# A hybrid decoder block on one core: how meta and x come in, and where the second residual is stored

## The chip, the cores and the metric

The kernel runs on one core of a Trainium2 chip. The core has a matrix engine (TensorE, PE in the profile), a vector engine (VectorE, DVE), a scalar engine (ScalarE, ACT), GpSimd (POOL), and the queues of SyncE (SP), ScalarE and GpSimd, from which transfers are started. The metric is device time in microseconds, the median of several runs. All times below are in microseconds where no unit stands.

## The reference

One layer works on 16 learned meta tokens followed by 256 tokens of x, each of 2048 channels. Everything is in float32. Cut to what matters:

```python
h = concatenate([meta, x])                       # 272 x 2048
u = rms_norm(h, g_pre_mix)
z_pool, v_conv, g_conv, gate_a, gate_b = split(u @ w_in)
y_a = causal_multiscale_pool(z_pool, w_pool_grp, pool_scale) @ w_pool_out
y_b = conformer_conv(v_conv, g_conv, w_dw, ...) @ w_conv_out
m = sigmoid(gate_a) * y_a + sigmoid(gate_b) * y_b
h = h + rms_norm(m @ w_o, g_post_mix)
u = rms_norm(h, g_pre_mlp)
h = h + rms_norm(square(relu(u @ w_up)) @ w_down, g_post_mlp)
return h without the meta tokens
```

## The kernel before, in words

**Precision.** A float32 product is made of three products of rounded parts. Each weight and each activation is split in a high part (a cast on ScalarE) and a low part, the residue (a subtraction on VectorE); high times high, high times low and low times high are added up in PSUM. So each weight chunk of 1 MB (128 x 2048) costs a transfer, a cast and a residue before TensorE can use it.

**The start.** Tokens have to stand in the free dimension and channels on partitions, so x and meta are turned by TensorE (a product with the identity, `ident`). At the start SP loads meta as 16 rows (`m_in`, L433), ScalarE's queue and SP load the first 512 columns of x in two halves of 128 tokens (L436), and then SP loads the first two weight chunks in pieces (`open_chunk`, L351), with the rest of x in three pieces of 512 columns between them (`X_BEHIND`, `load_x`). A third chunk follows whole. `DUMMIES` says how many turns of the identity onto itself `keep_warm` issues in three places. `meta_tiles` turns meta by sixteen products (L498), multiplies by the gain (L502) and splits it (L507, L508) in four parts, the first before the loop and three in it. `x_tile(k)` turns channel tile k, two products (L488), and splits it (L490 on ScalarE, L491 on VectorE). `pieces_to` splits the weights' rows for it (L356, L359). The first loop has sixteen steps, one for each channel tile, of six products (L534) each; tiles 0 to 2 are turned before it, and step k turns tile k + 3 behind its products. From step 5 on, every second step squares a piece of x or meta for the first norm (`sq_tile`, L516); the squares left over are planned. GpSimd's queue loads the taps and the parameter rows after the last piece of x is there (L442 to L444).

**The planned parts.** All that follows is put down as a list of items, each with an engine, a cost, and the names of what it reads and writes (`plan.add`). TensorE's order is given; from it each item gets a due time, and `order` plays the list through and has every engine take the ready item that is due first. The order that comes out is the program. The first plan holds everything up to the output projection `w_o`. Its weight chunks are split by `split_of` (L817 on ScalarE, L822 on VectorE), one whole chunk at a time. The second plan holds the MLP, with its own loads (L1773) and splits (L1800, L1805).

**Between the two plans** an order is written out by hand. It ends the last block of `w_o`, forms `norm1` for the two halves of 128 tokens (t = 0, 1), adds the residual block by block (`residual(t, n)`, L1501, four blocks of 512 columns for each t), turns the sum `h1` (`u2_tiles`, L1577, with casts L1583 and residues L1587), and makes the first products of `w_up` (`up_high`, `up_low`). The second plan then begins with eight squares of h1 (`square_h1`, L1495 on ScalarE) for the second norm, and a single transfer of h1 to DRAM (`keep_h1`, L1778, 2 MB, on SP's queue). Only after it can the room of h1 be used for weights (rooms 5 and 6). The copy in DRAM comes back near the end for the last residual (L2126).

Of the kernel before, what the change touches and what calls it, by code (L numbers as in the profile page):

```python
# [28 lines left out]
LAST_PIECE = "U1a0 U1a1 U1b0 U1b1 X1 X2 Y1 Y3 Y2 Y4 X3 X4"  # L29


DUMMIES = (11, 2, 1)
SQUARES_FROM = 5
AFTER_G0 = [("z", 0), ("z", 1), ("v", 1), ("z", 2), ("g", 1), ("v", 2), ("g", 2), ("z", 3),
            ("v", 3), ("g", 3)]
# [175 lines left out]
def hybrid_block(ctx: ExitStack, tc: tile.TileContext, ins: dict, out: bass.AP):  # L211
# [212 lines left out]
    def col(name, k):  # L424
        return vecs[:, cols[name] + k:cols[name] + k + 1]

    X_BEHIND = {(0, 4): 1, (0, 8): 2, (1, 4): 3}

    def load_x(b):
        sl = slice(b * CW, (b + 1) * CW)  # L430
        nc.sync.dma_start(x_in[:, :, sl], xv[:, :, sl])

    nc.sync.dma_start(m_in, meta)  # L433
    pre_rows = load_rows(nc.scalar, "g_pre_mix")
    for t, queue in enumerate((nc.scalar, nc.sync)):
        queue.dma_start(x_in[:, t, :CW], xv[:, t, :CW])  # L436
    for _ in range(FIRST + 1):
        open_chunk()
    ssq = const.tile([P, NT + 1, XB], F32, name="ssq")
    taps_in = big.tile([TAPS, CC], F32, tag="c", name="taps_in")  # L440
    nc.gpsimd.memset(ssq, 1.0)
    nc.gpsimd.tensor_copy(taps_in[:, :1], x_in[:TAPS, 0, D - 1:])  # L442
    nc.gpsimd.dma_start(taps_in, w_dw)
    other_rows = load_rows(nc.gpsimd, "pool_scale", "b_dw", "conv_ln_g", "conv_ln_b", "g_pre_mlp")  # L444
    warm_up(AF.Sqrt)
# [3 lines left out]
    def keep_warm(n):  # L449
        for _ in range(n):  # L450
            nc.tensor.transpose(idle[:, :P], ident, ident)
# [41 lines left out]
            op0=ALU.mult, op1=ALU.subtract)  # L493

    def meta_tiles():
        pt = acc_tile("mt_in")[:, :KD * M].rearrange("p (k m) -> p k m", k=KD)
        for k in range(KD):
            nc.tensor.transpose(pt[:, k, :], m_in[:, k * P:(k + 1) * P], ident[:M, :M])  # L498
# [3 lines left out]
        nc.vector.tensor_mul(mt, pt, vecs[:, g0:g0 + KD, None].broadcast_to([P, KD, M]))  # L502

        def part(ks, i):
            hi, lo = u.meta(ks, 0)[i], u.meta(ks, 1)[i]
            src = mt[:, ks.start:ks.stop - 1, :] if i == 0 else mt[:, ks.stop - 1, :]
            nc.scalar.copy(hi, src)  # L507
# [61 lines left out]
    meta_parts = meta_tiles()  # L569
    first_banks = acc_tiles("v0", HALF_CW // P)  # L570
    accs = [acc[:, :L] for acc in first_banks]
    squares = [(b, t) for b in range(XB) for t in range(NT + 1)]
    LEAD = 3

    def turn_and_split(k):
        if k < KD:
            x_tile(k)
        pieces_to(k + 1)

    meta_parts.pop(0)()  # L580
    keep_warm(DUMMIES[1])
    for k in range(LEAD):
        turn_and_split(k)
    keep_warm(DUMMIES[2])
    for k in range(KD):
        for j, acc in enumerate(accs):
            mm3(acc, *opened[k // HALF[0]][:2], u, (k % HALF[0], k), slice(j * P, (j + 1) * P),
                k == 0, k == KD - 1)
        turn_and_split(k + LEAD)
        if k < 3:  # L590
            meta_parts.pop(0)()
        if k >= SQUARES_FROM and k % 2 and k < KD - LEAD:
# [27 lines left out]
    def block(n):  # L620
        return slice(n * CW, (n + 1) * CW)
# [189 lines left out]

    def split_of(m_, q, rows):
        box, n = split_at[m_], slot0 + m_

        def high():
            box["flat"] = part_tile("hi", n)
            nc.scalar.copy(box["flat"], rooms[q]())  # L817
            box["hi"] = box["flat"].rearrange("p (k c) -> p k c", k=rows)

        def low():  # L820
            lo = part_tile("lo", n)
            nc.vector.tensor_sub(lo, rooms[q](), f32(box["flat"]))  # L822
            box["lo"] = lo.rearrange("p (k c) -> p k c", k=rows)
        return high, low

# [663 lines left out]

    norm1 = Norm("mix")  # L1490
    norm3 = Norm("mlp")

    def square_of(src, norm, t, n, scale=1.0):
        junk = tmp.tile([P, CW], F32, tag="junk", bufs=1, name=f"sq_{norm}_{n}_{t}")
# [5 lines left out]
    def residual(t, n):  # L1500
        nc.vector.scalar_tensor_tensor(  # L1501
            h1[:, t, block(n)], og[:, t, block(n)], norm1.r[:, t], h1[:, t, block(n)],
            op0=ALU.mult, op1=ALU.add)

    def m_of(k):
        return lambda part, ts_: m[:, k, part, ts_]
# [97 lines left out]
    def last_block(t):  # L1604
        last_factor(og[:, t, block(NB - 1)], last_o[t], NB - 1)
# [2 lines left out]
    norm1.finish(0)  # L1608
    for n in range(2):
        residual(0, n)  # L1610
    last_block(0)

    def both(parts):
        high, low = parts
        high()
        for i in range(CK):
            low(i)
# [8 lines left out]
    chain[0]()  # L1626
    high()
    residual(0, 2)
    for i, f in enumerate(chain[1:]):
        f()  # L1630
        low(i)
# [20 lines left out]

    up_high(0, 0)
    both(u2_tiles(0, 1, 2 * CK, CK))
    up_high(1, 0)
    parts_ = u2_tiles(1, 1, 0, CK)
    residual(1, 1)
    both(parts_)
    up_high(2, 0)
    both(u2_tiles(1, 1, CK, CK))  # L1660
    residual(1, 2)
    last_block(1)
    residual(1, 3)
    residual(0, 3)
    ups[2][2].pop(0)()
    up_high(0, 1)
    up_low(0)
# [44 lines left out]
    kept = dram.tile([P, NT, D], F32, name="kept")  # L1712
    H_ROOMS = (5, 6)

    banks = {"u0": acc_tile("bank_u0"), "u1": acc_tile("bank_u1")}
    for j in range(4):
# [53 lines left out]
    def load(r):  # L1770
        src, (rows, width) = source(*r)
        room = room_at[r] = free_rooms.pop(0)
        plan.add("SP", 3.15 if r[0][0] == "U" else 2.95, lambda: nc.sync.dma_start(  # L1773
            room_of[room].rearrange("p (k c) -> p k c", k=rows), src),
            writes=(f"raw{room}",))

    def keep_h1():
        nc.sync.dma_start(kept, h1)  # L1778
# [58 lines left out]
    last_use_order = list(uses)  # L1837


    ssq2 = const.tile([P, NT, NB], F32, name="ssq2")  # L1840
    r2 = const.tile([P, NT], F32, name="r2")
    box2 = {}

    def square_h1(t, n):
        return lambda: square_of(h1[:, t, block(n)], ssq2, t, n)

    def mean2():
        box2["v"] = v = tmp.tile([P, NT], F32, tag="tot", name="tot2")
# [240 lines left out]
                 writes=(f"x{j // 2}{j % 2}",))  # L2089
    loads()  # L2090
    for t in range(NT):
        for n in range(NB):
            plan.add("ACT", 0.92, square_h1(t, n), writes=("junk", "ssq2"))
    plan.add("SP", 6.0, keep_h1, reads=("ssq2",), writes=[f"raw{r}" for r in H_ROOMS])
    free_rooms += H_ROOMS
    loads()
    plan.add("DVE", 0.4, mean2, reads=("ssq2",), writes=("v2",))
# [143 lines left out]
```

## Time and profile before

| | us |
|---|---|
| median of three runs | 1182.91 |
| the three runs | 1181.7, 1182.91, 1183.52 |
| profiled execution | 1181.75 |
| its span, first to last instruction | 1179.6 |

The profiled execution is 2.15 longer than its span. TensorE is busy for 1167.2 of the span, VectorE for 1064.4, ScalarE for 706.8 and GpSimd for 62.3. The first product of the first loop starts at 8.03, the first product of the third weight chunk at 23.88; the hand-written order runs from about 492 to 530, and h1 is stored from 536.27 on.

In the timeline a row has the start, the length, the engine, the line, the operation, what it writes and reads, and how many alike are merged; a bracket has the idle time before it and what ended it. "PEld" is TensorE's loading of the stationary operand, "SPq" and "ACTq" are the issuing of transfers.

### The profile page before, as it was taken

What the parts mean: (1) busy time and instruction counts of PE and PEld (TensorE: products, weight loads), DVE (VectorE), ACT (ScalarE), POOL (GpSimd) and SP (SyncE); (2) the same over time, 40 slices, a digit from 0 to 9 for tenths busy, and PEclk for the clock granted to TensorE, in tenths of its full rate; (3) what the DMA queues carried; (4) which work ended last, traced back from release to release, by engine and by line L of the source; (5) the groups of instructions that cost most, each with busy time, mean ns of one, the idle gap of its engine ahead of it and who ended that gap; (6) DMA issues with size and microseconds to landing.
All of it is one profiled execution on the core that took longest, in us unless ns stands there. A gap on an engine that the chain in (4) does not pass through costs nothing.

```text
span 1179.6 us, 15795 instructions
## 1 busy us (share of the span) xinstructions
PE 1167.2 (99%) x6314; PEld 1013.1 (86%) x6314; DVE 1064.4 (90%) x1155; ACT 706.8 (60%) x718; POOL 62.3 (5%) x62
## 2 busy tenths in 40 slices
PE   9999999999999999999999999999999999999996
PEld 9999998788888888898888888888888888888885
DVE  6799999999998998688998998998989989989857
ACT  7634454556478666566776666666656756656542
POOL 1000000000000000000101001000000010010000
PEclk9999999999999999999999999999999999999998
DMA  9855356789767799449999999999999999999941
GB/s 316 265 179 179 108 179 173 233 278 297 220 194 247 208 353 293 151 149 347 253 320 234 249 316 256 250 290 244 301 262 229 339 240 248 318 241 242 337 143 71
DMA packets 185177, 287.57 MB, mean 244 GB/s; under 512 B 4769, under 2 KB 92257, under 8 KB 184192
## 3 DMA queue, kind: packets, MB, share of 16 engines
q1 hardware_dynamic: 160784, 236.40, 58.7%
q0 software_dynamic: 23856, 49.44, 23.3%
q8 instruction: 49, 0.80, 0.3%
q10 hardware_dynamic: 464, 0.73, 0.2%
q14 instruction: 24, 0.20, 0.0%
HBM read 282.36 MB, written 4.19 MB: 243 GB/s over the span
## 4 chain that ended last, share of the span: by engine, by line
PE 95%; DVE 3%; DMA 1%; issue 1%; ACT 0%; DVEq 0%; ACTq 0%
PE bank_u L539 18%; PE bank_k L1252 16%; PE acc_up L1979 13%; PE bank_u L545 9%; PE acc_v L1252 9%; PE bank_k L534 8%; PE bank_a L1979 7%; PE bank_b L1979 5%; PE acc_v L534 4%; PE acc_up L539 1%; DVE lo L822 1%; PE bank_u L1979 1%; PE acc_up L545 1%; DMA raw_k<-in_w_in_dram 1%; PE acc_v L1512 0%
## 5 line engine op out<-in xcount | busy, mean ns | idle before, releaser
L539 PE MATMUL bank_u<-m,hi 128*128 128x512 f32 x960 | 329.6, 390 | 0.0
L545 PE MATMUL bank_u<-m,lo 128*128 128x256 f32 x960 | 265.3, 276 | 0.0
L539 PEld LDWEIGHTS bank_u<-m,hi 128*128 128x128 f32 x960 | 180.2, 188 | 38.0
L817 ACT CAST hi<-raw_p 128x2048 fp32r<-128x2048 f32 x70 | 133.8, 1912 | 111.1 <-PE bank_k L1252 28.2
L1805 DVE TENSOR_TENSOR lo<-raw_m,hi 128x2048 fp32r<-128x2048 f32 x75 | 171.6, 2288 | 18.5 <-ACT hi L1800 17.3
L545 PEld LDWEIGHTS bank_u<-m,lo 128*128 128x128 f32 x960 | 180.2, 188 | 1.6
L1800 ACT CAST hi<-raw_m 128x2048 fp32r<-128x2048 f32 x75 | 143.5, 1913 | 60.8 <-PE bank_u L539 39.3
L822 DVE TENSOR_TENSOR lo<-raw_p,hi 128x2048 fp32r<-128x2048 f32 x70 | 159.7, 2286 | 12.9 <-ACT hi L817 12.6
L1979 PE MATMUL acc_up<-hi,forms 128*128 128x512 f32 x440 | 143.9, 390 | 0.0
L1805 DVE TENSOR_TENSOR lo<-raw_h,hi 128x2048 fp32r<-128x2048 f32 x43 | 98.4, 2288 | 12.7 <-ACT hi L1800 12.3
L1800 ACT CAST hi<-raw_h 128x2048 fp32r<-128x2048 f32 x43 | 82.2, 1911 | 39.9 <-PE bank_u L539 17.7
L952 DVE SCALAR_TENSOR_TENSOR c<-a,taps,c 128x256 f32<-128x256 f32 x240 | 100.2, 478 | 0.0
L1979 PEld LDWEIGHTS acc_up<-hi,forms 128*128 128x128 f32 x440 | 82.6, 188 | 18.1 <-ACT G L2004 0.4
L534 PE MATMUL bank_k<-u_um,hi 128*128 128x272 f32 x512 | 95.2, 287 | 0.0
L1252 PE MATMUL bank_k<-hi,u_um 128*128 128x512 f32 x280 | 88.8, 389 | 0.7 <-ACT sg L1301 0.7
L1979 PE MATMUL acc_up<-lo,forms 128*128 128x512 f32 x220 | 86.0, 391 | 0.0
L1979 PE MATMUL bank_a<-hi,forms 128*128 128x512 f32 (+1 forms) x256 | 81.9, 383 | 0.0
L534 PEld LDWEIGHTS bank_k<-u_um,hi 128*128 128x128 f32 x512 | 79.7, 188 | 0.0
L534 PE MATMUL bank_k<-u_um,lo 128*128 128x272 f32 x256 | 73.3, 287 | 0.0
L1800 ACT CAST hi<-raw_c 128x2048 fp32r<-128x2048 f32 x23 | 43.9, 1908 | 41.7 <-PE bank_u L539 36.8
L1805 DVE TENSOR_TENSOR lo<-raw_c,hi 128x2048 fp32r<-128x2048 f32 x23 | 52.6, 2287 | 13.2 <-ACT hi L1800 13.2
L1979 PE MATMUL bank_b<-hi,forms 128*128 128x512 f32 (+1 forms) x200 | 63.5, 381 | 0.0
(398 smaller groups left out, 2230.6 us busy)
## 6 DMA issues: line engine op xcount, KB each, us to landing
raw_p<-in_w_in_dram SPq DMA_DIRECT2D x30, 1024.0 KB, 5.6
raw_m<-in_w_down_dram SPq DMA_DIRECT2D x25, 1024.0 KB, 8.8
raw_m<-in_w_down_dram POOLq DMA_DIRECT2D x23, 1024.0 KB, 10.2
raw_h<-in_w_up_dram SPq DMA_DIRECT2D x20, 1024.0 KB, 8.3
raw_m<-in_w_up_dram SPq DMA_DIRECT2D x17, 1024.0 KB, 8.2
raw_h<-in_w_down_dram SPq DMA_DIRECT2D x17, 1024.0 KB, 9.0
raw_c<-in_w_down_dram SPq DMA_DIRECT2D x15, 1024.0 KB, 5.2
raw_k<-in_w_in_dram SPq DMA_DIRECT2D x14, 1024.0 KB, 8.2
```

The costliest lines, as they stand in the source:

```text
L534: nc.tensor.matmul(acc, w[:, k[0], cs], act[:, k[1], a, off:], start=first and n == 0, stop=last and n == 2)
L539: nc.tensor.matmul(acc.rearrange("p (a t) -> p a t", a=2)[:, :, ts], hi[:, k[0], cs], act[:, k[1], :, off + ts.start:off + ts.stop], start ...
L545: nc.tensor.matmul(acc[:, :T], lo[:, k[0], cs], act[:, k[1], 0, off:], start=False, stop=stop, skip_group_check=True)
L817: nc.scalar.copy(box["flat"], rooms[q]())
L822: nc.vector.tensor_sub(lo, rooms[q](), f32(box["flat"]))
L952: nc.vector.scalar_tensor_tensor(C_c()[:, q, :], A_a()[:, q, i:i + T], taps[:, q, i:i + 1], C_c()[:, q, :], op0=ALU.mult, op1=ALU.add)
L1252: nc.tensor.matmul(banks[bank], a_(k, part), box[w_][:, k, :], start=opens and k == 0 and i == 0, stop=ends_ and k == CK - 1 and i == 2, s ...
L1800: nc.scalar.copy(box["flat"], raw_in(room))
L1805: nc.vector.tensor_sub(lo, raw_in(room), f32(box["flat"]))
L1979: nc.tensor.matmul(acc, forms[h][:, f, k, a_, :], box[w_][:, k, cs], start=start and k == 0 and n == 0, stop=stop and k == KH - 1 and n == ...
```

## The change

- Meta is loaded first in a wide form, `m_wide`: 128 partitions, eight groups of 16 tokens, 2 x 128 channels each. Two turns take the place of sixteen. The narrow form, which the squares read, is loaded by GpSimd's queue ahead of the taps.
- x comes in eight pieces of 256 columns. The first piece is again two halves on two queues; seven others stand between the pieces of the first two weight chunks.
- Before the loop tiles 0 and 1 are turned, not three. Behind step 0 tiles 2 and 3 are turned, behind step 1 none, behind step 2 tiles 4 and 5, and from step 3 on tile k + 3 as before. Dummies: 12 at the start and 3 ahead of the loop; the third place is gone. The squares of meta go to the end of their list.
- In the first plan the product with number 1 has its weights split in two halves, two casts and two residues of 1024 columns.
- Between the plans, six of the eight squares of h1 and five stores (of one or two blocks each, on GpSimd's queue) stand in the hand-written order. The second plan keeps the last two squares, and the single store on SP is gone; the room of h1 is taken when the first load into it is issued.

```diff
-DUMMIES = (11, 2, 1)
+DUMMIES = (12, 3)
...
-    X_BEHIND = {(0, 4): 1, (0, 8): 2, (1, 4): 3}
+    X_COLS = CW // 2
+    X_BEHIND = {(0, 2): 1, (0, 4): 2, (0, 6): 3, (0, 8): 4, (1, 2): 5, (1, 4): 6, (1, 6): 7}
 
     def load_x(b):
-        sl = slice(b * CW, (b + 1) * CW)
+        sl = slice(b * X_COLS, (b + 1) * X_COLS)
         nc.sync.dma_start(x_in[:, :, sl], xv[:, :, sl])
 
-    nc.sync.dma_start(m_in, meta)
+    KM = P // M
+    m_wide = tmp.tile([P, KD // KM, P], F32, tag="v", bufs=5, name="m_wide")
+    nc.sync.dma_start(m_wide, meta.rearrange("m (c k p) -> k m c p", k=KM, p=P))
     pre_rows = load_rows(nc.scalar, "g_pre_mix")
     for t, queue in enumerate((nc.scalar, nc.sync)):
-        queue.dma_start(x_in[:, t, :CW], xv[:, t, :CW])
+        queue.dma_start(x_in[:, t, :X_COLS], xv[:, t, :X_COLS])
...
     nc.gpsimd.tensor_copy(taps_in[:, :1], x_in[:TAPS, 0, D - 1:])
+    nc.gpsimd.dma_start(m_in, meta)
     nc.gpsimd.dma_start(taps_in, w_dw)
...
-        for k in range(KD):
-            nc.tensor.transpose(pt[:, k, :], m_in[:, k * P:(k + 1) * P], ident[:M, :M])
+        for c in range(KD // KM):
+            nc.tensor.transpose(pt[:, c * P:(c + 1) * P], m_wide[:, c, :], ident)
...
-    squares = [(b, t) for b in range(XB) for t in range(NT + 1)]
+    squares = [(b, t) for b in range(XB) for t in range(NT)] + [(b, NT) for b in range(XB)]
     LEAD = 3
+    TURNS = {0: (2, 3), 1: (), 2: (4, 5)}
...
+    for k in range(2):
+        turn_and_split(k)
     keep_warm(DUMMIES[1])
-    for k in range(LEAD):
-        turn_and_split(k)
-    keep_warm(DUMMIES[2])
...
-        turn_and_split(k + LEAD)
+        for n in TURNS.get(k, (k + LEAD,)):
+            turn_and_split(n)
...
+        width = CK * CW // (2 if m_ == 1 else 1)
+        cuts = [slice(c, c + width) for c in range(0, CK * CW, width)]
...
-            nc.scalar.copy(box["flat"], rooms[q]())
+            for cs in cuts:
+                nc.scalar.copy(box["flat"][:, cs], rooms[q]()[:, cs])
...
-            nc.vector.tensor_sub(lo, rooms[q](), f32(box["flat"]))
+            for cs in cuts:
+                nc.vector.tensor_sub(lo[:, cs], rooms[q]()[:, cs], f32(box["flat"][:, cs]))
...
+    def square_h1(t, n):
+        square_of(h1[:, t, block(n)], ssq2, t, n)
+
+    def keep(t, n0, n1):
+        cs = slice(n0 * CW, n1 * CW)
+        nc.gpsimd.dma_start(kept[:, t, cs], h1[:, t, cs])
...
     for n in range(2):
         residual(0, n)
+    square_h1(0, 0)
+    keep(0, 0, 2)
     last_block(0)
...
     residual(0, 2)
+    keep(0, 2, 3)
...
     both(u2_tiles(0, 1, 2 * CK, CK))
+    square_h1(0, 1)
     up_high(1, 0)
     parts_ = u2_tiles(1, 1, 0, CK)
     residual(1, 1)
+    keep(1, 0, 2)
     both(parts_)
+    square_h1(0, 2)
     up_high(2, 0)
     both(u2_tiles(1, 1, CK, CK))
+    for n in range(2):
+        square_h1(1, n)
     residual(1, 2)
+    square_h1(1, 2)
     last_block(1)
     residual(1, 3)
     residual(0, 3)
+    keep(1, 2, 4)
+    keep(0, 3, 4)
...
     for t in range(NT):
-        for n in range(NB):
-            plan.add("ACT", 0.92, square_h1(t, n), writes=("junk", "ssq2"))
-    plan.add("SP", 6.0, keep_h1, reads=("ssq2",), writes=[f"raw{r}" for r in H_ROOMS])
+        plan.add("ACT", 0.92, lambda t=t: square_h1(t, NB - 1),
+                 reads=[f"raw{r}" for r in H_ROOMS], writes=("junk", "ssq2"))
```

More of the change, by code (lines that the diff above doesn't have):

```diff
@@ L495, in meta_tiles @@
     def meta_tiles():
-        pt = acc_tile("mt_in")[:, :KD * M].rearrange("p (k m) -> p k m", k=KD)
-        for k in range(KD):
-            nc.tensor.transpose(pt[:, k, :], m_in[:, k * P:(k + 1) * P], ident[:M, :M])
+        pt = acc_tile("mt_in")[:, :KD * M]
+        for c in range(KD // KM):
+            nc.tensor.transpose(pt[:, c * P:(c + 1) * P], m_wide[:, c, :], ident)
+        pt = pt.rearrange("p (k m) -> p k m", k=KD)
         g0 = cols["g_pre_mix"]
@@ L1491, in hybrid_block @@
     norm3 = Norm("mlp")
+    ssq2 = const.tile([P, NT, NB], F32, name="ssq2")
+    kept = dram.tile([P, NT, D], F32, name="kept")
+    H_ROOMS = (5, 6)
     def square_of(src, norm, t, n, scale=1.0):
@@ L1710, in hybrid_block @@
         room_of[2 + b] = raws.tile([P, CK * CW], F32, tag="raw", name=f"raw_m{b}")
-    kept = dram.tile([P, NT, D], F32, name="kept")
-    H_ROOMS = (5, 6)
     banks = {"u0": acc_tile("bank_u0"), "u1": acc_tile("bank_u1")}
@@ L1772, in load, with f, rooms_of_h1 @@
         room = room_at[r] = free_rooms.pop(0)
[L1773 to L1778, printed above, removed]
+        def f():
+            if room not in room_of:
+                rooms_of_h1()
+            nc.sync.dma_start(room_of[room].rearrange("p (k c) -> p k c", k=rows), src)
+        plan.add("SP", 3.15 if r[0][0] == "U" else 2.95, f, writes=(f"raw{room}",))
+    def rooms_of_h1():
         room = big.tile([P, len(H_ROOMS), CK * CW], F32, tag="k8", bufs=2, name="raw_h1")
@@ L1837, in hybrid_block @@
     last_use_order = list(uses)
-    ssq2 = const.tile([P, NT, NB], F32, name="ssq2")
     r2 = const.tile([P, NT], F32, name="r2")
     box2 = {}
-    def square_h1(t, n):
-        return lambda: square_of(h1[:, t, block(n)], ssq2, t, n)
     def mean2():
```

## The prediction

> **What bounds the kernel now.** I read the page first: shares of the engines, then the chain that ended last.
>
> ```profile
> span 1179.6 us, 15795 instructions
> PE 1167.2 (99%) x6314; PEld 1013.1 (86%) x6314; DVE 1064.4 (90%) x1155; ACT 706.8 (60%) x718; POOL 62.3 (5%) x62
> PE 95%; DVE 3%; DMA 1%; issue 1%; ACT 0%; DVEq 0%; ACTq 0%
> ```
>
> TensorE is busy for 99% of the span and carries 95% of the chain. So an edit gains only where TensorE stands idle, does work that is not needed, or runs slowly. The timeline shows such a place: the first ten microseconds. Columns: start, length, engine, line, tiles, count, and in brackets the idle time before.
>
> ```profile
> 1.20 0.40 SPq L436 DMA_DIRECT2D x_in<-in_x_dram  x1
> 1.35 2.61 PE L451 MATMUL idle<-ident 128*128 128x128 f32 x11 [1.35 <-POOL ident masks.py:199]
> 4.27 1.86 PE L498 MATMUL mt_in<-ident,m_in 16*128 16x16 f32 x16
> 6.06 0.69 PE L451 MATMUL idle<-ident 128*128 128x128 f32 x2
> 6.17 0.42 DVE L502 TENSOR_TENSOR mt<-mt_in,vecs 128x256 f32<-128x256 f32 x1 [1.53 <-PE mt_in L498]
> 6.54 1.49 PE L488 MATMUL xt<-ident,x_in 128*128 128x128 f32 x6
> 6.63 0.35 ACT L507 CAST u_um<-mt 128x192 fp32r<-128x192 f32 x1 [3.46 <-DVE mt L502]
> 7.21 0.47 ACT L490 ACTIVATE u_um<-xt,vecs 128x256 fp32r<-128x256 f32 x1 [0.23 <-PE xt L488]
> 7.58 0.40 ACT L356 CAST hi<-raw 128x256 fp32r<-128x256 f32 x1
> 7.72 0.48 DVE L491 SCALAR_TENSOR_TENSOR u_um<-xt,vecs,u_um 128x256 fp32r<-128x256 f32 x1 [0.35 <-ACT u_um L490]
> 8.03 0.82 PE L534 MATMUL acc_v<-u_um,hi 128*128 128x272 f32 x2
> 8.12 0.42 DVE L359 TENSOR_TENSOR lo<-raw,hi 128x256 fp32r<-128x256 f32 x1
> 9.51 0.39 PE L488 MATMUL xt<-ident,x_in 128*128 128x128 f32 x2
> ```
>
> The first product starts at 8.03. Until then TensorE does dummies (L451), sixteen meta turns (L498) and six turns of x (L488). What a step takes once all runs, from the chain in order of time, and where the next chunk's products begin:
>
> ```profile
> 20.36 0.22 PE xt L488 x2
> 20.58 0.75 PE acc_v L534 x6
> ...
> 23.88 0.29 PE L534 MATMUL bank_k<-u_um,hi 128*128 128x272 f32 x1
> ```
>
> Two turns take 0.22 and six products 0.75 there. At 6.54 six turns take 1.49, and the first six products fill 8.03 to 9.51: TensorE ran at half speed until about 9.3. (The lengths tell it; the windows below have 1.00 in their clock column there.)
>
> When the data came, from the DMA issues (size, then time from issue to landing):
>
> ```profile
> x_in<-in_x_dram SPq DMA_DIRECT2D x1, 256.0 KB, 4.4
> x_in<-in_x_dram ACTq DMA_DIRECT2D x1, 256.0 KB, 4.6
> m_in<-in_meta_dram SPq DMA_DIRECT2D x1, 128.0 KB, 3.2
> raw<-in_w_in_dram SPq DMA_DIRECT2D x1, 1024.0 KB, 10.6
> ...
> 2.00:4.00 2.00, 1.96 (x10) 1.56 (x8) 0.00 (x0) 1.16 (x2) 0.00 (x0) 1.00 0.76 164
> 4.00:6.00 2.00, 1.86 (x17) 1.86 (x17) 0.17 (x1) 0.00 (x0) 0.00 (x0) 1.00 1.03 334
> ```
>
> (The last two rows are windows: start and end, length, busy time of TensorE, its weight loads, VectorE, ScalarE and GpSimd, then clock, DMA share, GB/s.) Both x halves were issued at 1.20, so they were there at 5.6 and 5.8. The first turn of x waited 0.7 longer, for the meta turns and two dummies.
>
> **The start, step by step.** *Wide meta load.* The sixteen turns (1.86) become two of 128 columns, 0.21 each: 0.43, ready about 4.9 if the wide load lands as the narrow one did. Its cost is not in the trace: bounds are the narrow load's 3.2 less nothing, and the 4.4 of a 128-row load twice its size; I take 3.2, the same bytes. At 4.4 meta is turned by 5.6, and L502 and L507 (0.42, 0.35) then hold ScalarE until 6.4: 0.7 lost.
>
> *x in pieces of 256 columns.* Up to the first turn 256 KB less have to pass. At 334 GB/s that is 0.8, at the 164 of the first stretch 1.6; most of it passes after 4.0, so I take 0.9 and x near 4.9, with bounds 5.8 (latency alone) and 4.2. From the first turn to the first product is 8.03 - 6.54 = 1.49, made of the same rows in either kernel (two turns, L490, L356). L507 ends about 0.1 later than L490 wants. First product: 4.9 + 1.5 + 0.1 = 6.5, 1.5 earlier. The twelfth dummy (0.2) ends before the data, the three others run while ScalarE prepares: nothing.
>
> *The steps.* A step is six products (0.75) and a tile's turn (0.22). Sixteen steps and fourteen remaining turns are 12.0 + 3.1 = 15.1. Only two tiles are turned ahead, so VectorE's residues (L491 0.48, L359 0.42, behind L490 0.47 and L356 0.40) come late at steps 0, 2 and 4. From a tile's turn to its last residue these rows make about 1.8 (0.4 for the turn, 0.4 for L490 before L356 follows, 0.4 more, and the residues 0.6 behind). Counted from the first product: step 0 needs L359 at 0.5 and, by L359's row, stands 0.4 for it; with the turns of tiles 2 and 3 it ends at 1.6, step 1 at 2.35. Tile 2, turned from 1.15, is complete at 2.95, and step 2 wants it after two products, at 2.6: 0.35. Step 2 ends at 3.45; tile 4, turned there, is complete at 5.25, and step 4 wants it, behind two turns, step 3 and a turn, at 5.1: 0.15 to 0.2. 6.5 + 15.1 + 0.95 = 22.55, against 23.88: 1.3 saved. Bounds: 0.6 (half speed until 9.3, below) and 2.3 (no stalls).
>
> **What the head start meets.** TensorE is earlier, the transfers are not.
>
> ```profile
> GB/s 325 348 378 384 392 367 351 350 343 350 350 351 358 339 378 257 293 337 342 352 347 347 348 348 353 347 345 347 353 348 350 340 353 356 361 342 356 351 350 345
> 9.69 0.37 SPq L351 DMA_DIRECT2D raw<-in_w_in_dram  x1
> 24.66 1.91 ACT L817 CAST hi<-raw_s0a 128x2048 fp32r<-128x2048 f32 x1
> 26.60 4.71 DVE L822 TENSOR_TENSOR lo<-raw_s0a,hi 128x2048 fp32r<-128x2048 f32 x2 [0.89 <-ACT hi L817]
> 30.69 0.52 PE L534 MATMUL bank_k<-u_um,hi 128*128 128x272 f32 x2
> ```
>
> The rates run from 10 to 36 us in 40 slices: 380 while 2 KB rows of x pass, 350 on rows of 1 KB. All x now comes in 1 KB rows: 1.5 MB at 350 instead of 380 is 0.35 late. m_in (128 KB) on GpSimd's queue, ahead of taps and parameter rows, takes another 0.35 from the weights. So the first whole chunk lands at 9.69 + 10.6 = 20.3, then 21.0; its first quarter needs cast and residue, 1.2, and TensorE wants it at 22.55. Just covered; if that cover goes, each microsecond late costs one. Four more x issues on SP (0.40 each) delay nothing, since a chunk issued at 9.69 waits 10.6 for its turn.
>
> *Two halves.* The next chunk was cast at 24.66 and its residue done near 28.9, for 30.69. Now it is wanted at 29.4; with data 0.7 later it would be done at 29.6 whole, while in halves the first residue is there about 27.7. The extra instructions: 256 columns take 0.40 and 2048 take 1.91, so each costs 0.2 fixed on ScalarE, a like amount on VectorE, both idle just before. It saves the 0.2 that the head start would lose, no more. After this a chunk of 1 MB lands every 3 (350 GB/s) and feeds 48 products, 6.0: slack grows, and the head start lasts.
>
> **The second pass.**
>
> ```profile
> 506.00:519.00 13.00, 13.00 (x111) 12.82 (x110) 10.79 (x27) 6.68 (x19) 0.00 (x0) 1.00 0.00 1
> 525.00:550.00 25.00, 25.00 (x148) 22.00 (x147) 18.87 (x29) 20.00 (x36) 0.00 (x0) 1.00 1.02 371
> kept<-h SPq DMA_DIRECT2D x1, 2048.0 KB, 11.9
> 502.69 1.14 ACT L1583 ACTIVATE m<-ht,vecs 128x128 fp32r<-128x128 f32 x4 [2.68 <-PE ht L1577]
> 527.29 0.62 ACT L1495 ACTIVATE ng_offset=None)_0_0_4499<-h 128x512 f32<-128x512 f32 x1
> 525.48 1.91 ACT L356 CAST hi<-raw 128x2048 fp32r<-128x2048 f32 x1 [1.79 <-DMA raw<-in_w_up_dram]
> 527.42 2.29 DVE L359 TENSOR_TENSOR lo<-raw,hi 128x2048 fp32r<-128x2048 f32 x1 [1.33 <-ACT hi L356]
> 530.09 0.40 PE L539 MATMUL bank_u<-m,hi 128*128 128x512 f32 x1
> ```
>
> TensorE has no gap here. Six squares (0.62 and a readout) move from behind 527.29 into ScalarE's waits for turns, such as the 2.68 before 502.69; five stores on GpSimd replace one on SP and fall into a stretch with 1 GB/s. Loads behind the store start sooner, but TensorE waited for none. I take zero: it cannot gain where TensorE never stops, and a square that ran into its cast would cost up to its 0.8; that end stays in the range.
>
> **Sum.** The profiled execution took 1181.75, its span 1179.6 and 2.15 around it; it lies 1.16 below the median of 1182.91 and next to the fastest run, 1181.7. 1181.75 - 1.3 = 1180.4, 0.21% under the median.
>
> The half speed says something on that median. From 8.03 to 9.3 products came at half speed; were the switch 1 to 3 later, it would cost 0.5 to 1.5, an estimate from those rows, and the three runs span 1.8. The Trainium skill ("TensorE: Matmul & The Clock Gate", Part 1) says that the clock is set by free-running windows of about 3.4 us, so that the switch falls differently in each run; one trace can't show this. In the changed kernel TensorE has been busy almost without pause since 1.35, so I expect full speed by 6.5 and less spread.
>
> **Rivals.**
> (a) *The clock stays low until about 9.3.* For it: eleven dummies from 1.35 to 3.96 did not raise it by 6.54. Against: the sixteen narrow turns behind them leave TensorE mostly empty, and now they are gone. Then products from 6.5 to 9.3 run at half speed and half the head start is lost: 0.6 to 0.7 is left, 1181.1. The same skill page, in Part 4 (PE-mode transpose), states that transposes don't count as busy time; by it, dummies and turns would do nothing, and this rival would be the result. The trace leaves it open.
> (b) *The first chunk is late.* Landing at 22 or more instead of 21.0 eats 1 or more: 1181.4 to 1181.8, no change. The quoted rates speak against it, the GpSimd load ahead of it for it.
> (c) *Slower: stores before loads.* The last stores, of blocks finished late, meet the loads for the second pass. The chunk cast at 525.48 is wanted one chunk after 530.09, at 530.1 + 5.4 = 535.5; cast and residue take 4.2, so it decides from a landing at 531.3 on, 5.9 later than now. One store of 2 MB took 11.9 to land; if the loads stood behind it for all of that, the loss is 6 less 1.3: about 1186.4. Against: most blocks are ready well before 519, when the transfers were idle.
>
> **Chances.** Forecast 0.53 (own range 1179.3 to 1181.2, of which four fifths lie under 1180.5); (a) 0.25; (b) 0.13; (c) 0.09. 0.2% is 2.4, about what a measurement of this kernel can tell from no change: faster means under 1180.5, slower over 1185.3. Faster: 0.42 and a little from (a) with a favourable switch, 0.48; slower: most of (c), 0.08; the rest 0.44. The range 1178.9 to 1182.7 takes in the no-stall bound, (a) and (b), and leaves (c) out.
>
> **What would show it.** Right: first L534 near 6.5, meta turned twice by 5, L488 at 0.12 apart from its third turn on, first bank_k product near 22.6, no gap at its start; ScalarE's squares before 516, stores landed by 525, TensorE unbroken from 500 to 575. Wrong: L488 at 5.8 or later, half speed past 9, TensorE waiting for L356 of the chunk of 1 MB, or for the chunk after 530.

## The result, and the profile after

The changed kernel takes 1180.09 (median of 13 runs, 1179.23 to 1180.72), the kernel before, on the same chip, 1182.48 (13 runs, 1181.59 to 1184.02). The medians differ by 2.4; the ratio of the runs is 0.9978, with a 95% interval of 0.9971 to 0.9985, 0.22% faster. The profiled execution of the changed kernel took 1180.13, its span is 1178.3.

The page of the changed kernel: span, busy time of the engines, chain that ended last.

```profile
span 1178.3 us, 15808 instructions
PE 1165.8 (99%) x6301; PEld 1011.7 (86%) x6301; DVE 1064.0 (90%) x1156; ACT 707.3 (60%) x719; POOL 65.5 (6%) x68
PE 95%; DMA 2%; DVE 2%; issue 0%; ACT 0%; DVEq 0%; POOL 0%; ACTq 0%; POOLq 0%
```

TensorE still bounds the kernel. Its busy time fell by 1.4 (1167.2 before), which is about the difference of the two spans, 1.3. The start in the timeline (start, length, engine, line; in brackets the idle time before):

```profile
0.74 0.78 SPq L436 DMA_DIRECT2D m_wide<-in_meta_dram  x1
1.17 0.44 ACTq L439 DMA_DIRECT2D x_in<-in_x_dram  x1
1.36 2.82 PE L455 MATMUL idle<-ident 128*128 128x128 f32 x12 [1.36 <-POOL ident masks.py:199]
4.32 0.69 PE L502 MATMUL mt_in<-ident,m_wide 128*128 128x128 f32 x2
4.80 1.06 PE L492 MATMUL xt<-ident,x_in 128*128 128x128 f32 x4
5.04 0.42 DVE L507 TENSOR_TENSOR mt<-mt_in,vecs 128x256 f32<-128x256 f32 x1 [0.44 <-PE mt_in L502]
5.76 0.47 ACT L494 ACTIVATE u_um<-xt,vecs 128x256 fp32r<-128x256 f32 x1
6.13 0.39 ACT L356 CAST hi<-raw 128x256 fp32r<-128x256 f32 x1
6.58 0.71 PE L539 MATMUL acc_v<-u_um,hi 128*128 128x272 f32 x2
7.74 0.60 PE L492 MATMUL xt<-ident,x_in 128*128 128x128 f32 x4
8.09 0.50 PE L539 MATMUL acc_v<-u_um,hi 128*128 128x272 f32 x2
```

The first product starts at 6.58 instead of 8.03. Behind step 0 the turns begin only at 7.74. The chain, in order of time, shows the end of the first loop and the first products of the next chunk:

```profile
20.46 0.22 PE xt L492 x2
20.68 2.51 PE acc_v L539 x18
23.20 5.92 PE bank_k L539 x48
```

The timeline has that first bank_k product at 23.03:

```profile
23.03 0.41 PE L539 MATMUL bank_k<-u_um,hi 128*128 128x272 f32 x2
```

The kernel before has it at 23.88: of the 1.45 won at the first product 0.85 is left. In windows (TensorE's clock, DMA share and GB/s are the last three columns) the changed kernel has

```profile
4.00:6.00 2.00, 2.00 (x10) 1.86 (x10) 0.71 (x3) 0.50 (x2) 0.00 (x0) 1.00 0.87 240
6.00:8.00 2.00, 1.93 (x12) 1.47 (x11) 1.79 (x5) 1.19 (x4) 0.00 (x0) 1.00 0.88 288
22.00:24.00 2.00, 2.00 (x16) 1.83 (x15) 2.00 (x5) 1.91 (x4) 0.00 (x0) 1.00 1.06 154
```

and the kernel before, for the last of the three,

```profile
22.00:24.00 2.00, 2.00 (x16) 1.85 (x15) 1.60 (x5) 2.00 (x6) 0.00 (x0) 1.00 1.10 348
```

So the transfers run slower than before in three places: 240 instead of 334 GB/s at 4 to 6 us, 288 instead of 331 at 6 to 8, and 154 instead of 348 at 22 to 24. The last one falls on the load of the chunk that is split in halves:

```profile
27.16 2.00 ACT L826 CAST hi<-raw_s0a 128x1024 fp32r<-128x1024 f32 x2 [3.25 <-DMA raw_s0a<-in_w_in_dram]
28.24 2.36 DVE L832 TENSOR_TENSOR lo<-raw_s0a,hi 128x1024 fp32r<-128x1024 f32 x2 [3.36 <-ACT hi L826]
29.84 0.52 PE L539 MATMUL bank_k<-u_um,hi 128*128 128x272 f32 x2
```

Its data lands at 27.08 (23.90 before), its cast starts at 27.16 (24.66 before), and TensorE begins on it at 29.84 without a gap. In the hand-written order the squares and stores went where they were put:

```profile
501.16 0.63 ACT L1508 ACTIVATE ng_offset=None)_0_0_4167<-h 128x512 f32<-128x512 f32 x1 [1.70 <-DVE h L1514]
514.24 0.64 ACT L1508 ACTIVATE ng_offset=None)_2_1_4334<-h 128x512 f32<-128x512 f32 x1 [0.55 <-DVE h L1514]
515.83 1.21 POOL L1523 DMA_DIRECT2D kept<-h  x2 [5.59 <-DVE h L1514]
524.38 1.91 ACT L356 CAST hi<-raw 128x2048 fp32r<-128x2048 f32 x1 [1.38 <-DMA raw<-in_w_up_dram]
```

The first and the last of the six squares lie at 501 and 514, the last stores are issued at 515.83, and the chunk cast at 525.48 before is cast at 524.38.

Two more readings of the traces are used below. One is the trace's own record of TensorE's clock, which says when it rises from half to full speed. (The clock column of the windows follows this record and shows 1.00 ahead of its first entry, so before the first rise it says nothing: here the record has the rise at 7.03, and the rows above show 1.00 from 4 on.) The other is the time that TensorE loses in a stretch: its start-to-start distances, less the usual distance for the same shape (the 5th percentile of the trace), added up.

### The profile page after: what moved, and what is told of

The parts are those of the page before. It is cut to its first block, busy times and chain, and to the rows that moved or that the text cites. A ratio compares the mean times of both kernels' runs of the same rounds, so it can differ in the third digit from the quotient of the medians.

```text
span 1178.3 us, 15808 instructions
## 1 busy us (share of the span) xinstructions
PE 1165.8 (99%) x6301; PEld 1011.7 (86%) x6301; DVE 1064.0 (90%) x1156; ACT 707.3 (60%) x719; POOL 65.5 (6%) x68
## 4 chain that ended last, share of the span: by engine, by line
PE 95%; DMA 2%; DVE 2%; issue 0%; ACT 0%; DVEq 0%; POOL 0%; ACTq 0%; POOLq 0%
PE bank_u L544 18%; PE bank_k L1262 16%; PE acc_up L2005 13%; PE bank_u L550 9%; PE acc_v L1262 9%; PE bank_k L539 8%; PE bank_a L2005 7%; PE bank_b L2005 5%; PE acc_v L539 4%; PE acc_up L544 1%; DMA raw_k<-in_w_in_dram 1%; PE bank_u L2005 1%; DMA raw_p<-in_w_in_dram 1%; DVE lo L832 1%; PE acc_up L550 1%
```

## The experiments

My theory after the result: the start gives 0.85, and the halves save more than the 0.2 that I gave them, since the chunk behind is cast 2.5 late. First rival: half of the gain comes from the second pass (the stores by blocks). Second rival, about the clock: idle transposes do nothing, as rival (a) had it.

Times of the experiments are medians, measured in three groups, and each ratio is to the kernel before in the same group. It took 1183.01 in the first group (stores and squares, start and halves, whole weights the first time, moved meta load), 1182.97 in the second (no idle transposes, x in 512 columns, wide load alone, the first faster version) and 1182.73 in the third (the rest).

### Stores and squares alone

The kernel before, with this part of the change only:

```diff
+    square_h1(0, 0)
+    keep(0, 0, 2)
     last_block(0)
...
-    plan.add("SP", 6.0, keep_h1, reads=("ssq2",), writes=[f"raw{r}" for r in H_ROOMS])
```

> The kernel before with the stores by blocks and the moved squares alone. My prediction priced this part at nothing: then the time is that of the kernel before within 0.3 us, and TensorE loses between 525 and 600 us what it loses there before (0.57 + 0.29 + 0.41 us beyond its cadence in three stretches of 25 us). Rival, read from the trace after: this part is worth 0.6 us by itself, so the time is 0.6 us under the kernel before, and TensorE loses about 0.66 us between 525 and 600. The first product stays at 8.0 in both.

Measured: 1182.28, ratio 0.9995 (0.9986 to 1.0004). From 525 to 600 TensorE loses 0.57 + 0.28 + 0.23, 1.08, between the two expectations. The 0.57 lies in one chunk, from 541 to 551, where a part of the steps is 8 to 9 ns longer. It is there in both traces of the kernel before and in this one, and in none of those with the wide meta load. So it doesn't go with the stores; what it comes from is open. The stores by blocks make no difference that can be told from none; the interval allows a gain of 0.14%, 1.7 us. The first product comes at 7.79 here, not at 8.03, with the same code up to there: executions of one start differ by that much.

### The start and the halves alone

The changed kernel, with the one store on SP and the eight squares back in the plan (the other way round than above).

> The changed kernel with the one store of h on SP and the squares back behind it: the start and the two halves alone. By my prediction this part is the whole change: the time of the changed kernel, within 0.3 us. By the rival it is 0.6 us above the changed kernel (about 0.66 us lost becomes 1.27 us between 525 and 600). First product at 6.6, first bank_k product at 23.0 in both.

Measured: 1180.04, ratio 0.9974 (0.9964 to 0.9984), the changed kernel's time. So the first rival falls as far as medians go: start and halves carry the gain. One row of its timeline shows how much the start depends on the transfers:

```profile
12.45 0.41 PE L492 MATMUL xt<-ident,x_in 128*128 128x128 f32 x2 [0.83 <-DMA x_in<-in_x_dram]
```

A piece of x that landed at 10.92 in the changed kernel's trace landed at 12.32 here, with the same code to that point. TensorE waited, and the first bank_k product came at 23.96 instead of the expected 23.0. Nothing of the head start was left there, and this execution still took only 1180.54. From the first bank_k product to the end of the last product the fourteen traces of this document take 1144.5 to 1146.4, so a single trace can't weigh a head start of 0.85; the medians have to.

### The next chunk's weights whole, twice

```diff
-        width = CK * CW // (2 if m_ == 1 else 1)
+        width = CK * CW
```

> The changed kernel with the weights of the next chunk (the second of the first pass) cast and subtracted whole. My prediction gave the halves 0.2 us. The trace after says more: that chunk landed at 27.1, a whole cast of 1.9 and the first residue of 2.3 end near 31.4, and TensorE wants it at 29.8: 1.2 to 1.5 us lost in one gap ahead of the first product of that chunk, so 1.2 to 1.5 us above the changed kernel.

> The run with whole weights once more, beside the changed kernel on the same chip. If the 1.2 us that it lost ahead of the second chunk's residue products lasts to the end, the median lies 0.8 to 1.3 us above the changed kernel's; if a later wait that the changed kernel has and this one has not gives it back (as its first profile shows: 0.14 us lost at 225 to 250 instead of 1.42), 0.1 to 0.4 us above, which is what my prediction gave the halves.

Measured: 1180.35, ratio 0.9977 (0.9968 to 0.9986); the second time 1180.39, 0.9981 (0.9972 to 0.9989), beside 1179.63, 0.9974 (0.9964 to 0.9984), of the changed kernel in the same group. The first execution:

```profile
27.16 1.91 ACT L826 CAST hi<-raw_s0a 128x2048 fp32r<-128x2048 f32 x1 [2.85 <-DMA raw_s0a<-in_w_in_dram]
29.10 2.29 DVE L832 TENSOR_TENSOR lo<-raw_s0a,hi 128x2048 fp32r<-128x2048 f32 x1 [3.83 <-ACT hi L826]
31.45 0.39 PE L539 MATMUL bank_k<-u_um,lo 128*128 128x272 f32 x1 [0.74 <-DVE lo L832]
```

TensorE takes the high part from 30.19 on and then waits for the residue. From the first product of this chunk to the next chunk's is 7.04 (second time 7.03) instead of 6.03. In the place the halves are worth 1.0; over the whole kernel the medians lie 0.3 (above the changed kernel's median of another group) and 0.8 (of the same group) above, with intervals that overlap. That the 1.0 lasts to the end is not shown.

### Whole weights, with the narrow meta load moved

```diff
-    nc.gpsimd.dma_start(m_in, meta)
...
     loads()
+    nc.sync.dma_start(m_in, meta)
```

> As the run with whole weights, and the narrow meta load moved from GpSimd's queue to SP's, behind the early chunk loads. If the load of 16 rows of 8 KB on GpSimd's queue is what holds that chunk back until 27.1, the chunk lands by about 25.5 (the rate between 22 and 24 us is above 300 GB/s instead of 154), whole weights are ready near 29.8, and the time is that of the changed kernel within 0.4 us. If the small loads behind it (taps, parameter rows) or the later end of x hold it back, it lands after 26.5 and the time stays 0.8 us or more above the changed kernel.

Measured: 1179.56, ratio 0.9971 (0.9962 to 0.9980). The timeline:

```profile
25.78 1.91 ACT L825 CAST hi<-raw_s0a 128x2048 fp32r<-128x2048 f32 x1 [1.57 <-DMA raw_s0a<-in_w_in_dram]
27.72 2.29 DVE L831 TENSOR_TENSOR lo<-raw_s0a,hi 128x2048 fp32r<-128x2048 f32 x1 [2.55 <-ACT hi L825]
30.11 0.51 PE L538 MATMUL bank_k<-u_um,hi 128*128 128x272 f32 x2
```

The chunk lands 1.4 earlier than with that load on GpSimd's queue, the whole residue ends at 30.0, just ahead of TensorE at 30.11, and TensorE loses nothing. The rate between 22 and 24 is 299 GB/s instead of 154. So this load of 128 KB in 16 rows, in that place, is what made the halves needed. It slows the stream where it now runs, too (207 GB/s between 26 and 28, against 345 in the changed kernel). Whether its form or its place matters more wasn't tried: it was not loaded in another form.

### Without the idle transposes

```diff
-DUMMIES = (12, 3)
+DUMMIES = (0, 0)
```

> The changed kernel without its fifteen idle transposes. In four profiled runs of it or of its near variants the clock record rises at 4.89 to 7.03 us, the earliest with nothing but such transposes and two real turns behind it. If transposes raise the clock, then without them no stretch of 3.41 us is filled before the products begin at 6.6, the clock rises between 10.0 and 13.4, and products at half speed from 6.6 cost 1.0 to 2.5 us against the changed kernel (1181.1 to 1182.6 beside 1180.1). If they do not count, as rival (a) had it, nothing is lost: the same time within 0.3 us and a rise at 5 to 8 us as before.

Measured: 1180.94, ratio 0.9986 (0.9977 to 0.9994), 0.85 above the changed kernel's first median (another group) and a little less than I expected. The clock rises at 11.43, within the expected stretch. One thing I hadn't expected:

```profile
3.87 0.69 PE L502 MATMUL mt_in<-ident,m_wide 128*128 128x128 f32 x2 [1.08 <-DMA m_wide<-in_meta_dram]
6.12 0.82 PE L539 MATMUL acc_v<-u_um,hi 128*128 128x272 f32 x2 [0.60 <-ACT hi L356]
```

Meta is there at 3.87, and the first product comes 0.46 earlier than with the transposes. So the twelve transposes stand in the way of the turns by 0.45, and by this trace still more than pay for it through the clock: the first bank_k product comes at 24.28 here. (The intervals of the two kernels' ratios overlap.)

### x in pieces of 512 columns, and the wide meta load alone

The changed kernel with the old pieces of x:

```diff
-    X_COLS = CW // 2
-    X_BEHIND = {(0, 2): 1, (0, 4): 2, (0, 6): 3, (0, 8): 4, (1, 2): 5, (1, 4): 6, (1, 6): 7}
+    X_COLS = CW
+    X_BEHIND = {(0, 4): 1, (0, 8): 2, (1, 4): 3}
```

> The changed kernel with x in pieces of 512 columns, as before. My prediction charged the two halves of the first piece with 0.9 us on the way to the first turn: x lands at 5.3 to 5.6 instead of 4.6, the first product comes at 7.4 instead of 6.6, and the step stalls shrink (tiles 2 and 3 are there from the start), so 0.3 to 0.9 us above the changed kernel. Rival: the start is set by the late steps' data alone, the stalls give all of it back, and the first bank_k product stays within 0.2 us of 23.0.

And the kernel before with only the wide load and its two turns:

```diff
-    nc.sync.dma_start(m_in, meta)
+    nc.sync.dma_start(m_wide, meta.rearrange("m (c k p) -> k m c p", k=KM, p=P))
...
+    nc.gpsimd.dma_start(m_in, meta)
     nc.gpsimd.dma_start(taps_in, w_dw)
```

> The kernel before with the wide meta load alone (and the narrow one on GpSimd's queue for the squares), x and the order of the turns as before. By my working meta turned by 4.9 and x landing at 5.6 bring the first product to 7.3 instead of 8.03, without the stalls that turning only two tiles ahead makes: the first bank_k product near 23.1 instead of 23.88, 0.7 us under the kernel before. If x were as late as the narrow turns let TensorE free, nothing would be gained (within 0.3 us). The chunk behind has to be ready whole by 29.9; if m_in holds it back as in the run with whole weights, 0.5 to 1.2 us of this are lost again there.

Measured: 1182.02, ratio 0.9992 (0.9984 to 1.0001), and 1182.24, 0.9995 (0.9987 to 1.0004). Neither gains anything that can be told from nothing. The first one lost 1.9 to the changed kernel's first median, where I had expected 0.3 to 0.9. Its timeline:

```profile
6.11 0.47 PE L492 MATMUL xt<-ident,x_in 128*128 128x128 f32 x1 [1.09 <-DMA x_in<-in_x_dram]
8.17 0.82 PE L539 MATMUL acc_v<-u_um,hi 128*128 128x272 f32 x2
```

TensorE waits for x, the first product comes at 8.17 instead of 7.4, and the clock rises only at 10.25, although the twelve idle transposes ran as in the changed kernel. The first bank_k product comes at 25.32, 2.3 later than there: 1.6 at the first product, and by estimate 1.0 through half speed until 10.25 (half of 2.1), less what smaller stalls give back. My expectation had left the clock out. The second one's timeline, and its DMA issues in the first 8 us (size, time from issue to landing):

```profile
6.13 0.33 PE L491 MATMUL xt<-ident,x_in 128*128 128x128 f32 x1 [1.01 <-DMA x_in<-in_x_dram]
6.85 0.77 PE L491 MATMUL xt<-ident,x_in 128*128 128x128 f32 x5 [0.39 <-DMA x_in<-in_x_dram]
8.04 0.82 PE L538 MATMUL acc_v<-u_um,hi 128*128 128x272 f32 x2 [0.31 <-ACT hi L356]
```

```profile
x_in<-in_x_dram ACTq DMA_DIRECT2D x1, 256.0 KB, 4.9
x_in<-in_x_dram SPq DMA_DIRECT2D x1, 256.0 KB, 5.2
```

The changed kernel's, in the first 20 us:

```profile
raw<-in_w_in_dram SPq DMA_DIRECT2D x1, 1024.0 KB, 9.2
x_in<-in_x_dram ACTq DMA_DIRECT2D x1, 128.0 KB, 3.1
x_in<-in_x_dram SPq DMA_DIRECT2D x1, 128.0 KB, 3.0
```

Behind the narrow load x took 4.6 and 4.4; behind the wide one it takes 4.9 and 5.2, and its second half is issued at 1.59 instead of 1.20, since the wide load's issue is 0.78 long. So x comes at 6.1 and 6.8, not at 5.6 and 5.8, and what the wide load wins at the turns it loses at x: the first bank_k product, expected near 23.1, comes at 24.95. Only with x in halves of 128 KB (4.2 and 4.6) is the first product early. Whether small pieces of x would do with the narrow load wasn't tried, nor the new order of the turns by itself. The windows of the same run show the transfers behind the wide load (272 GB/s where the kernel before has 334) and the clock:

```profile
4.00:6.00 2.00, 1.11 (x5) 0.76 (x5) 0.85 (x3) 0.35 (x1) 0.00 (x0) 1.00 0.87 272
8.00:10.00 2.00, 1.96 (x9) 1.88 (x9) 2.00 (x6) 1.32 (x4) 0.00 (x0) 0.55 1.08 374
10.00:12.00 2.00, 2.00 (x12) 2.00 (x11) 0.90 (x3) 0.91 (x4) 0.00 (x0) 0.60 1.07 367
```

The record has a rise at 4.79, a fall at 8.21 and a rise at 11.62, each 3.41 behind the last. From 4.79 to 8.21 TensorE had long gaps (rows above; it was busy for 1.7 of the 3.41), and the products from 8.21 on ran at half speed.

### Both kernels once more

> The changed kernel once more, for a second profiled execution and more times. If the 1.05 us that TensorE loses at 233 to 242 us in its first profiled execution (a wait for VectorE's residues) belongs to the kernel, it is there again; if it belongs to the execution, it may be gone (0.2 us as in three variants). The clock rises somewhere between 4.8 and 8.2 us if it goes by windows of 3.41 us and any stretch full of transposes or products counts.

> The kernel before once more, for a second profiled execution: the clock rises between 7.9 and 11.6 us (narrow turns don't fill a window, so the first full one begins after 4.3 or so), and the time goes up by about half of what the rise comes later than 9.29. The 9 ns longer steps of one chunk at 541 to 551 us are there again if they belong to the program.

Measured: the changed kernel 1179.63 (8 runs, 1179.12 to 1180.77), ratio 0.9974 (0.9964 to 0.9984); the kernel before 1181.79 in its single execution. From the four traces:

```
                              before   again    changed  again
first bank_k product           23.88   23.96     23.03   23.10
clock rises at                  9.29    9.53      7.03    6.42
lost by TensorE, 225 to 250     1.14    1.31      1.42    0.26
lost in one wait near 624       0       0         0       1.06
end of the last product      1169.89 1169.92   1168.62 1169.05
time of the execution        1181.75 1181.79   1180.13 1180.56
```

The head start of 0.85 is the same in both pairs. It also lasts: in the first pair the last products end 1.27 apart, in the second 0.87. The loss at 225 to 250 belongs to the execution, not to the changed kernel: it was gone the second time, and another of the same size stood near 624. That one stands in three more traces (1.0 to 1.5): without idle transposes, in the first faster version, and with whole weights the first time, while the second time with whole weights it is gone. The waits of the two executions of the changed kernel, each in its stretch (total, times, longest):

```profile
PEld acc_v L1262 <- DVE lo L832: 1.4, 2, 0.9
```

```profile
PEld bank_u L544 <- DVE F_raw L1910: 1.2, 1, 1.2
```

Both times TensorE waits for VectorE. Near 624 VectorE is behind on a chunk that landed at 618.3; in a run without that loss (the last one below), it landed at 616.8. At 225 to 250 the landing alone doesn't tell: the chunk landed at 235.75 in the trace that lost 1.42, and at 235.82 in the second one with whole weights, which lost about 0.2. The three traces with the narrow meta load lost 1.0 to 1.3 at 225 to 250; of the eleven with the wide one, one lost that much (1.42), the others 0.14 to 0.67. Why it tends that way wasn't found out.

### Two versions meant to be faster

Halves kept, the narrow meta load behind the chunk loads (as in the run above), the first weight row cast ahead of meta's cast; and the same with ten transposes at the start:

```diff
+    pieces_to(1)
     meta_parts.pop(0)()
...
-DUMMIES = (12, 3)
+DUMMIES = (10, 3)
```

> The changed kernel with two more edits: the narrow meta load behind the early chunk loads on SP's queue, and the first weight row cast by ScalarE ahead of the meta cast. ScalarE is idle from 3.1 to 5.5 and the row lands at 5.03, so its cast (0.40) leaves the way of the first product: 6.2 instead of 6.6. If ScalarE's order is what holds the first product, the first bank_k product comes 0.2 to 0.4 us earlier and the time is 1179.2 to 1179.8; if the stalls at steps 2 and 4 (data of the third row at 8.5) give it back, the time is that of the run with the meta load behind, 1179.6, within 0.2 us.

> The changed kernel with the meta load behind the chunk loads, the first weight row cast first, and ten idle transposes instead of twelve ahead of the parameter turn (they end at 3.7 instead of 4.2; the run without any turned meta at 3.87 instead of 4.32). If TensorE's order was holding the start, the first product comes at 5.9 to 6.1; if the third step's data (landed at 8.5 to 9.0) binds, the first bank_k product stays at 23.0 to 23.4 and the time at 1179.6 within 0.3 us.

Measured: 1179.78, ratio 0.9974 (0.9963 to 0.9985), and 1179.19, 0.9973 (0.9962 to 0.9983). The second one's start:

```profile
4.04 0.69 PE L501 MATMUL mt_in<-ident,m_wide 128*128 128x128 f32 x2
6.16 0.91 PE L538 MATMUL acc_v<-u_um,hi 128*128 128x272 f32 x2 [0.49 <-ACT u_um L493]
```

The first product is at 6.29 and 6.16, the first bank_k product at 23.43 and 22.98: 0.4 won at the first product is nearly all given back by the steps behind, which want data (x for the third step landed at 7.8 and 7.6, its weights at 9.0 and 8.5). Both beat the kernel before; neither is shown to beat the changed one.

## Why the prediction was right or wrong

*The time.* 1180.4 was forecast and 1180.09 measured; faster was the likeliest case. That the two numbers lie so near is in good part luck. The sum took its 1.3 from a profiled execution of 1181.75, which lies 0.7 under the median of thirteen runs, 1182.48; taken from that median it gives 1181.2. The median fell by 2.4, nearly twice the 1.3, and the sum did not come out term by term either.

*First product, 6.5.* Measured 6.58 and 6.63. Two terms behind it were off, in opposite ways. Where TensorE waited for meta, it was there at 3.87, 4.04 and 4.54 (three runs; 3.1 to 3.8 from issue, for the estimate of 3.2). In the changed kernel's first trace it did not wait, so "the twelfth dummy ends before the data" was wrong there: the twelve transposes and the turn of the parameter row hold meta's turns until 4.32. x was charged with 0.9 less than the 5.8 of before; the wide load in front of it costs it 0.5 to 1.0, and the smaller pieces bring 1.9 and 2.2 (6.1 and 6.8 against 4.2 and 4.6; 4.6 and 4.9 in the second trace). The small price of x in halves, and the wide load at no cost to x, were both mis-sized.

*The steps, 22.55.* Measured 23.03. The three stalls were 0.41, 0.55 and 0.25 (step 0 takes 1.16; steps 1 and 2 together 2.05; step 4 1.08, where 0.75 to 0.83 is usual), 0.2 to 0.3 more than the 0.95 in all. The larger part is an error of the sum: the last three steps, behind which nothing is turned, take 2.6 (20.44 to 23.03), where I put three times 0.75, 2.25. They take 2.57 in the kernel before too (21.31 to 23.88). I set a time that was added up from rows against a time that was measured, and so counted 0.3 as saved that neither kernel has. With 22.9 in its place, 1.0 would have been forecast as saved; 0.85 was.

*The chunk behind.* The first whole chunk, forecast to land at 21.0, landed at 21.6 (issued at 12.48, 9.2 later), and TensorE did not wait for it. Rival (b) did not come, and its price was wrong: in three runs the chunk landed at 22.0 to 22.1 without a wait. For the next chunk "data 0.7 later" was 3.2 later (27.08 against 23.90). Two steps failed here. One is the price of m_in on GpSimd's queue, 0.35 by its bytes: with that load moved the chunk landed 1.4 earlier (25.70). The rate fell to 154 instead of 348 GB/s over two microseconds, and GpSimd's queue began later, since it waits for the last piece of x. The other is the price of x in small pieces, 0.35: the first whole chunk, which comes ahead of m_in, landed 1.4 later than before (21.6 against 20.3), and with the old pieces of x, at 19.8. Without m_in, too, the next chunk was 1.8 late. So the halves were worth 1.0 in their place, not 0.2.

*The second pass, zero.* This held: the run with stores and squares alone and the run without them differ from their bases by less than the measurement tells. Rival (c) did not come; the last stores went out at 515.83, and TensorE ran on.

*The clock.* The forecast "full speed by 6.5" was 7.03 and 6.42, and 4.87 to 6.36 in the six other runs with the transposes, the wide meta load and small pieces of x; so 6.5 was one of many possible times. The lesser spread came as well: 1.5 over 13 runs, against 2.4 (and 1.7 over 8 runs, against 2.8 over 21, the second time). Rival (a) fell: in the run of the start and the halves the clock rose at 4.89, when TensorE had done nothing but turns, most of them idle ones. The Trainium skill ("TensorE: Matmul & The Clock Gate", Part 1) says that the clock goes by free-running windows of about 3.41 us. The traces agree: rise, fall and rise at 4.79, 8.21 and 11.62, and from the rise to the fall at the end of the changed kernel's trace 1163.945, which is 341 times 3.4133. The same page of the Trainium skill says in Part 4 that transposes don't count as busy. For these 128x128 float32 turns the runs say otherwise, with a rise at 4.89 behind twelve of them and at 11.43 without. They have to fill nearly a whole window, though. In all fourteen traces TensorE was busy for 3.26 or more of the 3.41 ahead of a rise. In the window one earlier it was busy for 2.06 where the clock rose at 10.25 (x in 512 columns), and for 2.81 where it rose at 11.43 (no idle transposes), and neither of these raised it. The sixteen narrow turns of the kernel before are another matter: from 4.27 on they kept TensorE busy by the profile, so that the window from 2.46 to 5.88 had 3.24, and the clock did not rise before 9.29 (9.53 the second time).

*The median.* The profiled pairs differ by 1.6 and 1.2, the medians by 2.4 and 3.1. About 0.3 of each lies outside the span: the time is 2.06 to 2.18 longer than the span in every execution of the kernel before beside the experiments, and 1.73 to 1.83 in every one of the changed kernel. The run with stores and squares alone has 1.73 to 1.84, the one with start and halves alone 1.74 to 1.82, the one with the wide load alone 2.09 to 2.20; it goes with the program, and what sets it is open. The sum had taken it as the same for both kernels. The head start makes 0.85. The rest of the medians' difference, 1.2 and 1.9, is for the most part in no trace (0.4 in the first pair, nothing in the second): both profiled executions of the kernel before lie at the low end of its times. Its clock rose at 8.82, 9.29 and 9.53 in three traces with the old start, and the first bank_k product came at 23.51, 23.88 and 23.96; but in the first of them the first product, too, was 0.24 earlier, so only the other two tell of the clock. A rise that comes later still would cost half of the delay. By windows of 3.41 that is 1.7 at most, and the times of the kernel before spread over more (1181.5 to 1185.64 in 30 runs). So the clock can be a part of the rest; it is not shown, and it is not all of the spread.

## What to carry to other kernels

Set a sum of rows only against a sum of the same rows for the kernel before, never against a measured time; an error that is in both then cancels. A load of few, long rows can cost the main stream far more than its bytes (here 1.4 instead of 0.35), so price it by the stretch in which it runs and ask who waits there. Parts of a start (load form, piece size, order, idle work for the clock) hold or fall together: here the wide load alone gained nothing, and neither did all of the start without the small pieces of x. Compare medians with medians: a sum that starts from one profiled execution can meet the median by luck.

## What the runs showed of the hardware

- Idle 128x128 transposes raise TensorE's clock where little idle time lies between them and the work behind. Without them it rose at 11.43 instead of 4.9 to 7.0; with them and a wait of 1.1 for x behind, at 10.25; with gaps between 4.79 and 8.21 it fell again, and products ran at half speed until 11.62.
- The issue of a load with many short rows (the wide meta load) takes 0.78 on SP, where the others beside it take 0.4 to 0.5. With x in 512 columns behind it, 272 GB/s were moved between 4 and 6 (two traces), against 291 to 360 in three traces with the narrow load, and 378 and 380 between 6 and 8, against 306 to 344.
- 128 KB in 16 rows of 8 KB, beside the small loads behind it on GpSimd's queue, left between 147 and 229 GB/s of 348 between 22 and 24 (six traces with small pieces of x). Moved to SP's queue the same load went with 200 to 207 GB/s between 26 and 28 (three traces), and the chunk that had suffered landed 1.4 earlier.
- The same code can lose about 1 us in a wait in one execution and nothing in the next (1.42 and 0.26 at 225 to 250, 0 and 1.06 near 624), and a program's time outside of its span can differ by 0.3 from another's (2.06 to 2.18 against 1.73 to 1.83).
